# Feed-forward gate and up: one 512-column matmul for both parts of the activations, its halves added on the way out of PSUM

## The chip, the core and the metric

The kernel runs on one core of a Trainium2 chip. The metric is the device time of one execution in microseconds (us), the median of several. The engines named here are TensorE (PE, with its weight loads PEld), VectorE (DVE), ScalarE (ACT), GpSimd (POOL) and SyncE (SP), which issues the loads of the weights.

## The reference, cut to what matters

Two identical layers work on 256 tokens of 1024 channels in float32. Each layer is a feed-forward half step, a mixer of three branches, and a second feed-forward half step:

```python
D_MODEL, SEQ, DEPTH, D_FF = 1024, 256, 2, 2816

def swiglu(x, w_gate, w_up, w_down):
    return (jax.nn.silu(x @ w_gate) * (x @ w_up)) @ w_down

# in each layer
x = x + 0.5 * swiglu(rmsnorm(x, g1), ffn1_gate, ffn1_up, ffn1_down)
x = x + mixers(rmsnorm(x, g_mix))      # sparse attention, S5, dilated attention
x = x + 0.5 * swiglu(rmsnorm(x, g2), ffn2_gate, ffn2_up, ffn2_down)
```

The change touches gate and up of the four feed-forward stages.

## The kernel before

Every float32 product is made of rounded parts. A value is split into a high part, the copy that ACT writes as fp32r, and a low part, the difference that DVE or POOL writes; `mm3` (L105) then adds high times high, high times low and low times high in one PSUM accumulation, three matmuls for each pair of operands.

The weights come as a stream of units of 512 KB. `load_unit` (L206) loads a unit into one of four buffers `raw` by SP; `emit_unit` (L213) has ACT copy it to `wh` (L221) and DVE subtract it to `wl` (L228). There are five buffers each of wh and wl, and `unit()` (L233) sees to it that four units beyond the one in use have been asked for. In the feed-forward stages all wl are DVE's.

`ffn` (L332) goes through D_FF = 2816 in eleven blocks j of 256. Block 0 takes tokens as stationary operand (`tok_mm`). In blocks 1 to 10 the channels are stationary: `chan_mm` (L303) takes two units, each with four of the eight 128-row pieces of the 1024 inputs, and runs over the two halves c of 128 columns. It puts both halves into one PSUM bank "mm" of 512 float32 columns, the first 256 for c = 0, the others for c = 1; each half takes 8 x 3 matmuls of 256 columns (the 256 tokens), with a piece of wh or wl stationary and hTh or hTl, the high and low part of the normalised and transposed activations, moving. One call makes the gate, one the up projection. ACT takes the silu of the gate's bank in one instruction of 512 columns (L367), DVE multiplies the up bank by it (L369), and the product is split into ah by ACT (L370) and al by POOL (L371). Two blocks later `down` multiplies it by w_down into four accumulators (banks "pt" and "sc"), with moving operands of 512 columns. There are two buffers "mm".

In FFN1 `side(j)` adds steps of the set-up of the S5 branch: tables on POOL (L549 to L551), products on POOL (L570, L572) and on DVE (L538 to L540, L576, L578), transposes and small matmuls on PE (L562, L586, L597, L599). These have a lower priority. DVE also computes the parameters of S5 early in layer 0, with one long operation on POOL among them (L444, sp_r).

The order of the instructions on each engine is fixed when the program is built: a scheduler works on the instructions with their priorities and its own notion of their durations. On the chip each engine then takes its instructions in that order, and an instruction that waits holds up those behind it on its engine.

## Time and profile before

| | |
|---|---|
| median of 3 runs | 1362.7 us (1361.65 to 1364.24) |
| profiled execution, its own time | 1364.48 us |
| its span | 1362.7 us |
| mean granted clock of TensorE, share of full speed | 0.994 |
| busy share: PE / DVE / ACT / POOL | 98% / 62% / 51% / 35% |
| HBM read and written | 244.92 MB, 18.58 MB |

The span runs from the first to the last instruction of the profiled execution, and the time of the execution has 1.8 us more around it. A busy share is a mean over all stages of both layers. The four feed-forward stages lie at about 14 to 218 us (FFN1 of layer 0), 504 to 692 (its FFN2), 693 to 893 (FFN1 of layer 1) and 1171 to 1359. Times in rows are counted from the start of the span; a row of a timeline gives the start, the duration, the engine and the line, and in brackets how long the engine had been idle before it and which instruction released it.

### The profile page before, as it was taken

Reading aid. Unit: us, or ns where it says so; the run is one execution under the profiler, and the core shown is the slowest. Engines: PE = TensorE matmul, PEld = TensorE weight load, DVE = VectorE, ACT = ScalarE, POOL = GpSimd, SP = SyncE. Lnnn points to the kernel's source line nnn. Section 1 sums busy time; section 2 is a strip of 40 time slices with the busy share of each in tenths; the row PEclk is TensorE's granted clock in tenths of the full one; section 3 lists DMA queues with packets and bytes.
Section 4 is the critical chain, followed back from the end, with each engine's and each line's share of the span. In section 5 each row is a group of like instructions: output and inputs, shape, how many; then the busy total and the mean of one; then the engine's idle time right before and its main releaser. Section 6 shows DMA issues by size and latency. Waiting matters only on the chain.

```text
span 1362.7 us, 25418 instructions
## 1 busy us (share of the span) xinstructions
PE 1333.8 (98%) x10120; PEld 1257.6 (92%) x10120; DVE 842.1 (62%) x1166; ACT 700.7 (51%) x1018; POOL 474.4 (35%) x333
## 2 busy tenths in 40 slices
PE   8999999999999999999999999999999999999998
PEld 7998997999899979999999999889999999899997
DVE  5696955996434475444586579569864437644443
ACT  5444445687544545444544444456767345444442
POOL 0386514454236531111056125153442556111110
PEclk8999999999899999999999999999999999999999
DMA  8866767666557656666766766676666576466662
GB/s 251 239 197 216 251 213 218 196 184 185 145 157 220 186 176 195 185 186 186 217 187 202 222 202 215 226 231 177 187 199 174 165 220 197 154 189 186 186 186 93
DMA packets 246327, 265.69 MB, mean 195 GB/s; under 512 B 51136, under 2 KB 224192, under 8 KB 246208
## 3 DMA queue, kind: packets, MB, share of 16 engines
q1 hardware_dynamic: 245488, 261.44, 64.0%
q10 hardware_dynamic: 720, 2.62, 0.6%
q8 instruction: 79, 1.29, 0.4%
q14 instruction: 40, 0.33, 0.1%
HBM read 244.92 MB, written 18.58 MB: 193 GB/s over the span
## 4 chain that ended last, share of the span: by engine, by line
PE 76%; DVE 8%; DMA 6%; POOL 5%; ACT 2%; issue 2%; SPq 1%; POOLq 0%; ACTq 0%; DVEq 0%
PE mm L108 18%; PE mm L106 17%; PE mm L107 17%; DVE wl L228 3%; PE pt L108 3%; PE pt L107 3%; PE pt L106 3%; PE sc L108 2%; PE sc L107 2%; PE sc L106 2%; DMA raw<-in_w_in_dram 2%; DMA raw<-in_ffn_gate_dram 1%; ACT wh L221 1%; DMA raw<-in_ffn_down_dram 1%; PE p L900 1%
## 5 line engine op out<-in xcount | busy, mean ns | idle before, releaser
L228 DVE TENSOR_TENSOR wl<-raw,wh 128x1024 fp32r<-128x1024 f32 (+3 forms) x376 | 471.8, 1262 | 338.2 <-ACT wh L221 334.0
L221 ACT ACTIVATE wh<-raw 128x1024 fp32r<-128x1024 f32 (+2 forms) x396 | 414.4, 1048 | 456.9 <-PE mm L107 234.8
L108 PE MATMUL mm<-hTh,wl 128*128 128x256 f32 x1728 | 490.5, 284 | 0.0
L107 PE MATMUL mm<-hTl,wh 128*128 128x256 f32 x1728 | 489.5, 283 | 0.0
L106 PE MATMUL mm<-hTh,wh 128*128 128x256 f32 x1728 | 489.1, 283 | 0.0
L106 PEld LDWEIGHTS mm<-hTh,wh 128*128 128x128 f32 x1728 | 326.6, 189 | 2.2
L107 PEld LDWEIGHTS mm<-hTl,wh 128*128 128x128 f32 x1728 | 325.2, 188 | 1.6 <-issue 0.3
L108 PEld LDWEIGHTS mm<-hTh,wl 128*128 128x128 f32 x1728 | 325.8, 189 | 0.3 <-issue 0.3
L371 POOL TENSOR_TENSOR al<-aa,ah 128x512 fp32r<-128x512 f32 x40 | 68.2, 1706 | 466.1 <-ACT ah L370 466.1
L230 POOL TENSOR_TENSOR wl<-raw,wh 128x384 fp32r<-128x384 f32 (+2 forms) x108 | 144.9, 1347 | 199.6 <-ACT wh L221 166.9
L106 PE MATMUL mm<-wh,hTh 128*128 128x256 f32 (+1 forms) x496 | 143.8, 291 | 0.3 <-ACT hTh L282 0.3
L107 PE MATMUL mm<-wl,hTh 128*128 128x256 f32 (+1 forms) x496 | 142.2, 288 | 0.0
L108 PE MATMUL mm<-wh,hTl 128*128 128x256 f32 (+1 forms) x496 | 141.8, 290 | 0.0
L106 PEld LDWEIGHTS mm<-wh,hTh 128*128 128x128 f32 x496 | 94.8, 191 | 1.4 <-ACT hTh L282 0.5
L107 PEld LDWEIGHTS mm<-wl,hTh 128*128 128x128 f32 x496 | 94.5, 191 | 1.0 <-issue 0.3
L108 PEld LDWEIGHTS mm<-wh,hTl 128*128 128x128 f32 x496 | 93.7, 191 | 1.0 <-issue 0.3
L225 POOL TENSOR_TENSOR wl<-raw,wh 128x512 fp32r<-128x512 f32 x40 | 56.6, 1434 | 51.4 <-ACT wh L221 51.4
L107 PE MATMUL pt<-wl,ah 128*128 128x512 f32 x144 | 56.8, 395 | 1.5 <-DVE wl L228 1.5
L108 PE MATMUL pt<-wh,al 128*128 128x512 f32 x144 | 57.3, 398 | 0.0
L108 PE MATMUL sc<-wh,al 128*128 128x512 f32 x144 | 56.5, 392 | 0.0
L106 PE MATMUL pt<-wh,ah 128*128 128x512 f32 x144 | 56.4, 392 | 0.0
L107 PE MATMUL sc<-wl,ah 128*128 128x512 f32 x144 | 56.3, 391 | 0.0
(311 smaller groups left out, 2073.7 us busy)
## 6 DMA issues: line engine op xcount, KB each, us to landing
raw<-in_w_in_dram SPq DMA_DIRECT2D x100, 512.0 KB, 4.0
raw<-in_ffn_gate_dram SPq DMA_DIRECT2D x88, 512.0 KB, 4.3
raw<-in_ffn_up_dram SPq DMA_DIRECT2D x88, 512.0 KB, 4.6
raw<-in_ffn_down_dram SPq DMA_DIRECT2D x88, 512.0 KB, 4.1
raw<-in_w_out_dram SPq DMA_DIRECT2D x16, 512.0 KB, 3.8
Gd<-xh SPq DMA_DIRECT2D x8, 512.0 KB
Ad<-xl SPq DMA_DIRECT2D x8, 512.0 KB, 4.4
x<-Ad SPq DMA_DIRECT2D x8, 512.0 KB, 4.7
```

Of the source, the lines that this page charges most:

```text
L106: PE.matmul(o, lh, rh, start=start, stop=False)
L107: PE.matmul(o, lh, rl, start=False, stop=False)
L108: PE.matmul(o, ll, rh, start=False, stop=stop)
L221: A.activation(hv, r, AF.Copy)
L225: G.tensor_tensor(lv[:, :, cs], r[:, :, cs], hv[:, :, cs].bitcast(F32), op=ALU.subtract)
L228: V.tensor_tensor(lv[:, :, :c], r[:, :, :c], hv[:, :, :c].bitcast(F32), op=ALU.subtract)
L230: G.tensor_tensor(lv[:, :, c:], r[:, :, c:], hv[:, :, c:].bitcast(F32), op=ALU.subtract)
L371: G.tensor_tensor(al, a, ah.bitcast(F32), op=ALU.subtract)
L900: PE.matmul(bu[:, 32 * g:32 * g + 32], At[:, P * g:P * g + P], U[:, g], start=True, stop=True)
```

## The change

`new_h` makes one tile with the high and the low part of the activations behind each other, so that for each 128-row piece one access pattern [128, 2, 256] reads both. `wide_mm` takes the place of `chan_mm`. It asks for both units first and then runs over the halves c, with a bank of its own for each. For each of the eight pieces it issues one matmul of 512 columns with wh stationary, high and low part moving, into the two halves of the bank, and one of 256 columns with wl stationary and the high part moving into the first half. `gate_out` and `up_out` add the two halves as they leave the bank: an ACT copy of the second half to SBUF, a DVE add of the first; then the silu of 256 columns, or the multiply, in SBUF. In a block that is 64 matmuls for gate and up where there were 96. Each unit is used by two passes. Block 0, down and the mixer stay as they were. In the code after, lines above L250 keep their numbers, the S5 lines are 24 higher (L576 is L600, L578 is L602, L445 is L469).

```diff
     def new_h():
-        return [sb([P, KD, SEQ], F32R, "hTh"), sb([P, KD, SEQ], F32R, "hTl")]
+        both = sb([P, 2, KD, SEQ], F32R, "hT")
+        return [both[:, 0], both[:, 1], None, both]
...
         if t == 1:
-            h.append(last)
+            h[2] = last
...
+    def wide_mm(h, evac):
+        us = [unit() for _ in range(2)]
+        for c in range(2):
+            pq = ps("mm")
+            for kk in range(KD):
+                wh, wl = us[kk // 4]
+                cs = slice(c * P, (c + 1) * P)
+                PE.matmul(pq.rearrange("p (i t) -> p i t", i=2), wh[:, kk % 4, cs], h[3][:, :, kk, :],
+                          start=kk == 0, stop=False)
+                PE.matmul(pq[:, :SEQ], wl[:, kk % 4, cs], h[0][:, kk, :], start=False, stop=kk == KD - 1)
+            evac(c, pq[:, :SEQ], pq[:, SEQ:])
...
-                    pg = chan_mm(h)
-                    A.activation(s, pg, AF.Silu)
-                    pu = chan_mm(h)
-                    V.tensor_tensor(a, pu, s, op=ALU.mult)
+                    def gate_out(c, p0, p1):
+                        A.activation(s[:, c], p1, AF.Copy)
+                        V.tensor_tensor(s[:, c], p0, s[:, c], op=ALU.add)
+                        A.activation(s[:, c], s[:, c], AF.Silu)
+
+                    def up_out(c, p0, p1):
+                        A.activation(a[:, c], p1, AF.Copy)
+                        V.tensor_tensor(a[:, c], p0, a[:, c], op=ALU.add)
+                        V.tensor_tensor(a[:, c], a[:, c], s[:, c], op=ALU.mult)
+
+                    wide_mm(h, gate_out)
+                    wide_mm(h, up_out)
```

The shorter block also gives the scheduler other times, and so the order changes on every engine. Three places follow; the numbers in the names count buffers and differ between the two programs.

PE after, FFN1 of layer 0, block 3: the end of the gate's half c = 0 (bank mm_156), down matmuls of a unit wh_154 and wl_155, and the start of the half c = 1 (mm_157).

```order
L328 MATMUL mm_156_727<-hT_24_124,wl_115_561 128x256
L326 MATMUL mm_156_727<-hT_24_124,wh_114_560 128x512
L328 MATMUL mm_156_727<-hT_24_124,wl_115_561 128x256
L106 MATMUL pt_71_336<-wh_154_723,ah_73_338 128x512
L106 MATMUL sc_70_335<-wh_154_723,ah_73_338 128x512
L106 MATMUL pt_72_337<-wh_154_723,ah_73_338 128x512
L107 MATMUL pt_71_336<-wl_155_724,ah_73_338 128x512
L108 MATMUL pt_71_336<-wh_154_723,al_74_339 128x512
L107 MATMUL sc_70_335<-wl_155_724,ah_73_338 128x512
```

Before, down came after the whole of gate and up; now a part of it stands between the halves of the gate.

DVE in FFN1 of layer 0, around the operation that takes POOL's sp_r (L445, now L469). Before:

```order
L228 TENSOR_TENSOR wl_115_608<-raw_104_536,wh_114_607 128x1024
L462 TENSOR_SCALAR sp_k_131_683<-sp_k_131_683 128x64
L470 TENSOR_TENSOR sp_k_131_683<-sp_im_126_673 128x64
L471 TENSOR_TENSOR sp_den_134_700<-sp_den_134_700,sp_k_131_683 128x64
L472 RECIPROCAL sp_den_134_700<-sp_den_134_700 128x64
L228 TENSOR_TENSOR wl_150_760<-raw_107_566,wh_149_759 128x1024
L228 TENSOR_TENSOR wl_153_790<-raw_110_599,wh_152_789 128x1024
L445 TENSOR_SCALAR sp_xr_128_678<-sp_xr_128_678 128x64
```

After, with the wl of the down unit above as the last row:

```order
L228 TENSOR_TENSOR wl_115_561<-raw_100_458,wh_114_560 128x1024
L469 TENSOR_SCALAR sp_xr_131_637<-sp_xr_131_637 128x64
L228 TENSOR_TENSOR wl_118_567<-raw_105_504,wh_117_566 128x1024
L470 TENSOR_TENSOR sp_r_133_641<-sp_r_133_641,sp_xr_131_637 128x64
L228 TENSOR_TENSOR wl_152_718<-raw_108_510,wh_151_717 128x1024
L490 TENSOR_TENSOR sp_zs_135_652<-sp_r_133_641,sp_zs_135_652 128x64
L492 TENSOR_TENSOR sp_zs_135_652<-sp_r_133_641,sp_zs_135_652 128x64
L514 TENSOR_TENSOR r8_9_77<-sp_r_133_641 128x64
L228 TENSOR_TENSOR wl_155_724<-raw_113_558,wh_154_723 128x1024
```

Before, 19 wl of the program stood ahead of that operation; now there are 16.

DVE in FFN1 of layer 1, blocks 1 to 3. Before, a part with nothing but wl and the multiplies of blocks 1 and 2:

```order
L228 TENSOR_TENSOR wl_1314_8111<-raw_1297_8008,wh_1313_8110 128x1024
L369 TENSOR_TENSOR aa_1292_7976<-mm_1300_8039,silu_1291_7975 128x512
L228 TENSOR_TENSOR wl_1317_8141<-raw_1301_8040,wh_1316_8140 128x1024
L228 TENSOR_TENSOR wl_1321_8173<-raw_1304_8070,wh_1320_8172 128x1024
L228 TENSOR_TENSOR wl_1324_8203<-raw_1312_8108,wh_1323_8202 128x1024
L228 TENSOR_TENSOR wl_1327_8236<-raw_1315_8138,wh_1326_8235 128x1024
L369 TENSOR_TENSOR aa_1310_8106<-mm_1318_8169,silu_1309_8105 128x512
```

After, a part of the same blocks (the stretch from wl_1331 to wl_1386 has twelve wl, four L600 and two L602):

```order
L600 TENSOR_TENSOR xl_1441_8201<-s5C1_1375_7829,s5Q_1403_7989 128x1024
L602 TENSOR_TENSOR xh_1440_8200<-xh_1440_8200,xl_1441_8201 128x1024
L228 TENSOR_TENSOR wl_1359_7738<-raw_1340_7631,wh_1358_7737 128x1024
L228 TENSOR_TENSOR wl_1362_7744<-raw_1349_7683,wh_1361_7743 128x1024
L384 TENSOR_TENSOR silu_1347_7681<-mm_1356_7715,silu_1347_7681 128x256
L600 TENSOR_TENSOR xh_1475_8395<-s5C0_1374_7828,s5Q_1403_7989 128x1024
L389 TENSOR_TENSOR aa_1348_7682<-mm_1363_7747,aa_1348_7682 128x256
L600 TENSOR_TENSOR xl_1476_8396<-s5C1_1375_7829,s5Q_1403_7989 128x1024
L390 TENSOR_TENSOR aa_1348_7682<-aa_1348_7682,silu_1347_7681 128x256
L602 TENSOR_TENSOR xh_1475_8395<-xh_1475_8395,xl_1476_8396 128x1024
L228 TENSOR_TENSOR wl_1367_7792<-raw_1352_7689,wh_1366_7791 128x1024
```

The S5 products L600 and L602 moved here from blocks 5 to 9, and stand ahead of wl and of the adds that free the banks.

## Rows read from the trace of the kernel before

**Rows 1.** The page's first part: busy us, share, instructions.

```profile
PE 1333.8 (98%) x10120; PEld 1257.6 (92%) x10120; DVE 842.1 (62%) x1166; ACT 700.7 (51%) x1018; POOL 474.4 (35%) x333
```

**Rows 2.** Windows, one FFN2 block of layer 0; columns as named in the first line.

```profile
core 0: us, PE busy (x) PEld busy (x) DVE busy (x) ACT busy (x) POOL busy (x), PEclk, DMA share, GB/s
551.00:568.00 17.00, 17.00 (x123) 16.02 (x122) 8.04 (x7) 7.37 (x9) 1.81 (x1) 1.00 0.64 185
```

**Rows 3.** Windows, stretches of FFN1 in layer 0 and layer 1.

```profile
62.00:79.00 17.00, 17.00 (x122) 16.02 (x122) 16.90 (x44) 7.49 (x10) 7.45 (x10) 1.00 0.48 136
...
712.00:723.00 11.00, 11.00 (x95) 11.00 (x94) 11.00 (x7) 5.01 (x7) 11.00 (x6) 1.00 0.75 232
...
828.00:847.00 19.00, 19.00 (x165) 17.67 (x163) 18.04 (x12) 9.27 (x12) 10.44 (x5) 1.00 0.69 226
```

**Rows 4.** Timeline of PE, 256-column matmuls: start us, us, engine, line, operation.

```profile
130.08 0.28 PE L106 MATMUL mm<-hTh,wh 128*128 128x256 f32 x1
...
134.04 0.28 PE L106 MATMUL mm<-hTh,wh 128*128 128x256 f32 x1
```

**Rows 5.** Timeline of PE, 512-column matmuls of down.

```profile
102.03 0.39 PE L106 MATMUL pt<-wh,ah 128*128 128x512 f32 x1
...
104.31 0.39 PE L107 MATMUL sc<-wl,ah 128*128 128x512 f32 x1
```

**Rows 6.** Tile silu: duration in ns, min/median/max, of each form.

```profile
L367 ACT ACTIVATE silu<-mm x40: 575/579/599, 33.8 to 1339.1; 128x512 f32<-128x512 f32 x40
L369 DVE TENSOR_TENSOR aa<-mm,silu x40: 675/691/693, 39.8 to 1342.6; 128x512 f32<-128x512 f32 x40
L356 ACT ACTIVATE silu<-mm x8: 378/382/385, 23.6 to 1182.1; 128x256 f32<-128x256 f32 x8
L357 DVE TENSOR_TENSOR aa<-mm,silu x8: 414/417/427, 26.4 to 1183.8; 128x256 f32<-128x256 f32 x8
```

**Rows 7.** Groups of DVE, FFN2, 551 to 636 us: count, busy us, mean ns.

```profile
L228 DVE TENSOR_TENSOR wl<-raw,wh 128x1024 fp32r<-128x1024 f32 x30 | 36.7, 1225 | 41.1 <-ACT wh L221 40.6
```

**Rows 8.** Groups of DVE, FFN1 of layer 1, 706 to 733 us.

```profile
L228 DVE TENSOR_TENSOR wl<-raw,wh 128x1024 fp32r<-128x1024 f32 x11 | 22.2, 2045 | 0.7 <-ACT wh L221 0.7
...
L364 DVE TENSOR_TENSOR al<-y,ah 128x512 fp32r<-128x512 f32 x1 | 0.7, 678 | 0.0
L558 DVE TENSOR_TENSOR s5D<-s5D,cm 128x128 f32<-128x128 f32 x1 | 0.5, 544 | 0.0
```

**Rows 9.** Timeline of DVE, S5 products in FFN1 of layer 0.

```profile
107.44 2.99 DVE L576 TENSOR_TENSOR xh<-s5C,s5Q 128x1024 f32<-128x1024 f32 x1
112.87 2.29 DVE L576 TENSOR_TENSOR xh<-s5C,s5Q 128x1024 f32<-128x1024 f32 x1 [2.43 <-POOL tab L551]
...
119.77 1.22 DVE L576 TENSOR_TENSOR xl<-s5C,s5Q 128x1024 f32<-128x1024 f32 x1
```

**Rows 10.** Timeline of DVE in layer 1, the wl behind block 0's multiplies.

```profile
707.74 3.71 DVE L228 TENSOR_TENSOR wl<-raw,wh 128x1024 fp32r<-128x1024 f32 x2
```

**Rows 11.** Timeline of PE: first gate matmuls of block 3 (layer 0), block 1 (layer 1).

```profile
55.12 0.28 PE L106 MATMUL mm<-hTh,wh 128*128 128x256 f32 x1
...
704.73 0.28 PE L106 MATMUL mm<-hTh,wh 128*128 128x256 f32 x1
```

**Rows 12.** Timeline of DVE, the operation that takes POOL's sp_r.

```profile
60.59 1.28 DVE L445 TENSOR_SCALAR sp_xr<-sp_xr 128x64 f32<-128x64 f32 x1 [2.13 <-POOL sp_r L444]
```

**Rows 13.** Timeline of POOL, FFN1 of layer 0.

```profile
50.00 10.56 POOL L444 TENSOR_TENSOR sp_r<-sp_eb,sp_xr 128x64 f32<-128x64 f32 x1 [5.05 <-DVE sp_xr L441]
...
85.31 2.94 POOL L570 TENSOR_TENSOR xl<-s5b,s5Q 128x1024 f32<-128x1024 f32 x1
...
111.55 1.28 POOL L551 TENSOR_TENSOR tab<-xh,xl 128x512 f32<-128x512 f32 x1
```

**Rows 14.** Timeline of PE, its waits in FFN1 of layer 0.

```profile
119.91 0.50 PE L107 MATMUL pt<-wl,ah 128*128 128x512 f32 x1 [0.76 <-DVE wl L228]
...
122.49 0.50 PE L107 MATMUL pt<-wl,ah 128*128 128x512 f32 x1 [0.76 <-DVE wl L228]
```

**Rows 15.** The page's fifth part, ACT's copies of the weights.

```profile
L221 ACT ACTIVATE wh<-raw 128x1024 fp32r<-128x1024 f32 (+2 forms) x396 | 414.4, 1048 | 456.9 <-PE mm L107 234.8
```

## The prediction

> **What bounds the kernel now.** I read the busy shares first: PE is busy 98% of the span, DVE 62%, ACT 51% [rows 1]. Then I read the same shares stage by stage, because a mean says nothing of a stage. In the second feed-forward stage (FFN2) of a layer a block of 17.00 us has PE busy for all of it, DVE for 8.04 and ACT for 7.37 [rows 2]: PE alone bounds it, and nothing else is near. In the first stage (FFN1), which carries the S5 set-up as side work, PE is full too, but DVE is busy 16.90 of 17, 11.00 of 11 and 18.04 of 19 in the stretches shown [rows 3]. There DVE is a second bound just below the first, and it makes the low parts of the weights (wl, L228) without which PE can't go on. So the change has two halves with opposite signs: what it takes from PE counts in all four stages, what it adds to DVE counts where DVE has no room.
>
> **What PE gains.** Eleven triples of three 256-column matmuls take 134.04 - 130.08 = 3.96 us, 0.360 a triple and 0.120 a matmul [rows 4]. Ten 512-column matmuls take 104.31 - 102.03 = 2.28 us between the starts shown, 0.228 each [rows 5]. The new pair (one wide, one narrow) costs 0.228 + 0.120 = 0.348, so a pair saves 0.0125 (0.2275 taken for the wide). Gate and up of one block have 2 x 2 x 8 = 32 pairs, there are 10 changed blocks in each of 4 stages, hence 1280 pairs and **-16.0 us**. The trace has no matmul whose moving side reads two separate runs of 256, as the wide one does. Its bounds are the 0.2275 of a plain 512 and 0.240, two 256s, at which the gain is nothing; columns alone (512 / 2.4 GHz = 0.2133) would give -34. I take 0.2275, the row with the same number of columns.
>
> The Trainium skill's "TensorE: Matmul & The Clock Gate" (Back-to-back issue gap) puts the pitch of a warm matmul at N/2.4 ns plus about 2.5. By that a pair saves 2.5 ns against a triple, and the gain is an estimated 3.2 us instead of 16. The rows disagree: 0.120 and 0.2275 lie 13 and 14 ns above streaming.
>
> **What the way out costs.** One silu of 512 (0.579) and one multiply of 512 (0.691) become, for each half, a PSUM copy and a silu of 256 on ACT beside the up copy (0.382 by the 256-column silu), and two adds and a multiply of 256 on DVE (0.417 by the 256-column multiply) [rows 6]. ACT: 6 x 0.382 - 0.579 = +1.7 us a block; DVE: 6 x 0.417 - 0.691 = +1.8. In FFN2 that is DVE 9.9 and ACT 9.1 of 16.6: hidden. The banks too: each half has its own, and the order puts nine down matmuls (9 x 0.2275 = 2.0 us) or a whole other half between two uses. I cost it at nothing in FFN2; without that cover it would be the 1.2 us of copy, add and silu per half. New_h as one tile and the moved h[2] cost nothing.
>
> **What it costs in FFN1.** The scheduler answers the shorter blocks by placing the S5 side work earlier, and DVE runs strictly in the order that front shows.
>
> *Layer 1, blocks 1 to 3.* Between the wl named 1331 and the one named 1386 DVE now has 12 wl, 12 of the new 256-wide operations, four L600 and two L602 (L576 and L578 before) and two small ones. Before, this stretch had no L576 or L578. A wl takes 1.225 us alone [rows 7] but 2.045 here, where POOL computes beside it [rows 8]; L576 took 2.99 and 2.29 beside POOL, 1.22 alone [rows 9]. Sum: 12 x 2.045 = 24.5, 12 x 0.417 = 5.0, 4 x 2.29 = 9.2, 2 x 1.22 = 2.4, small ones 0.68 + 0.54 [rows 8], together 42.3. It starts at 707.74 [rows 10], so wl 1386 is there at 750.0 less the last two small operations, 749.2. PE starts block 1 at 704.73 [rows 11] and reaches the first matmul that wants wl 1386 after nine half passes of 8 x 0.348 (25.0), 27 down matmuls at 0.2275 (6.1) and 20 transposes at not over 0.12 (2.4): 738.2. PE waits **+11.0 us** in all. With wl and L600 at 1.22, as without POOL, DVE would be done at 735.0 and the wait is nothing; with L600 behind POOL's last table as well it is some 13.
>
> *Layer 0, blocks 3 to 5.* DVE's L445 waits until 60.59 for POOL's sp_r [rows 12], which takes 10.56 us from 50.00 [rows 13]. Before, 19 wl stood ahead of it, now 16 (as L469). So the wl of the down unit that PE wants between the two gate halves of block 3 comes three wl and four small operations behind that wait: 60.6 + 1.3 + 3 x 1.22 + 0.7 = 66.2. PE, which started block 3 at 55.12 [rows 11], would be there at 54.3 + 2.8 + 0.7 = 57.8. That is 8 us, or 4 if POOL can start sp_r some 4 us earlier because DVE's inputs for it no longer stand behind L558. In block 4 the wl of the next down unit stands behind three other wl and four S5 products of DVE; two or three of these at the 2.3 to 3.0 us of rows 9 in place of 1.22 make it up to 5 late. In block 5 an L600 waits for POOL's last table, which was ready at 111.55 + 1.28 = 112.8 and now has two more L570 of up to 2.94 ahead of it [rows 13]; behind that L600 stands an add which frees the bank that PE wants. PE is late by then, so 0 to 5. Sum 4 to 18; I take **+11**, and take off the 1.5 that PE already lost here [rows 14].
>
> *Later blocks of both layers.* 18.04 + 1.8 = 19.8 of DVE stands against 18.6 of PE [rows 3], 1.2 us in each of two such blocks: **+2.5**, between 0 and 7.
>
> **Sum.** -16.0 + 11.0 + 11.0 - 1.5 + 2.5 = +7.0 on the profiled execution's 1364.5, so 1371.5. That execution lies 1.8 above the median of the runs, 1362.7; on the median it is 1369.7, and I forecast **1370**. SP's weight loads move with the buffers that they fill and are cheap (DMA share 0.64 in rows 2); POOL's al waits for ACT as before.
>
> **Rivals.**
> (A) *The cover holds: faster, about 1351.* DVE is slow beside POOL only while POOL reads; if POOL's chain ends early or its turns fall elsewhere, wl costs 1.225 and the wait in layer 1 goes to 0, in layer 0 to the 4 us of sp_r: -16 + 4 = -12, 1351. For it: rows 7, and that PE lost only two gaps of 0.76 in the old schedule [rows 14] although DVE was full. Against it: POOL has the same chain to run, two products earlier. It decides below some 1.4 us a wl.
> (B) *The wide matmul saves nothing: about 1384.* If its two runs are read like two matmuls the pair costs 0.360, or if the fixed part is small the saving is a few us; the stalls shrink little with blocks that stay long: 1362.7 + 23 - 2 = 1384, the 2 being five stalled blocks whose PE time is 0.4 longer. Against it: the 512-column rows [rows 5]; nothing in the trace has that pattern. The skill's page named above would put it within 3 us of this.
> (C) *FFN2 stalls too: about 1382.* A weight unit now serves two passes and is given back one pass later; ACT's copy of the next (1.05 us) already waits for PE in 235 us of the profile [rows 15], and then DVE needs 1.22. Walking the block with these durations leaves about 1 us at the two tightest units. If each is 0.3 us late, 20 blocks x 0.6 = 12 more. For it: the margin was several us before. Against it: DVE and ACT have 40% free there [rows 2].
>
> **How the numbers follow.** A measurement of this kernel can tell some 0.2% from no change, so the borders are 1360.0 and 1365.4. The forecast has 0.50, its own range 1362 to 1378 (net stalls of 15 to 31 against the gain of 16): 0.46 slower, 0.04 same. A has 0.32 with a range of 1347 to 1364: 0.25 faster, 0.07 same. B has 0.06, C 0.12, both slower. Faster 0.25, same 0.11, slower 0.64. As cases of both signs hold the chance, the range for 8 in 10 reaches into A and into C: 1349 to 1384.
>
> **What would show it.** Right, if the profile after has pairs at 0.348 and FFN2 blocks of 16.6 us, and PE gaps released by DVE's wl or by the adds of L384 and L389 in FFN1, near 58 to 66, 80 to 120 and 712 to 752 us, some 20 in sum. FFN2 blocks of 17.0 speak for B, of 17.2 or gaps behind ACT's wh in FFN2 for C. Wrong about FFN1 if PE shows no gaps there and wl stands at 1.2 to 1.4. The least sure step is layer 0, where three waits hang on one another.

## The result and the profile after

| | before | after |
|---|---|---|
| median | 1362.81 us (1361.65 to 1364.24, 4 runs) | 1405.97 us (1404.06 to 1407.5, 4 runs) |
| ratio | | 1.0299, 95% interval 1.028 to 1.0318 |
| span of the profiled execution | 1362.7 us | 1405.1 us |
| mean granted clock, share of full speed | 0.994 | 0.983 |

The change makes the kernel 3.0% slower, 43 us. The direction was forecast, the size was not: 1370, with 1384 as the upper end.

The first part of the profile page of the kernel after, to be read beside [rows 1]:

```profile
PE 1348.8 (96%) x8840; PEld 1201.4 (86%) x8840; DVE 910.8 (65%) x1366; ACT 758.6 (54%) x1218; POOL 469.4 (33%) x333
```

PE has 1280 matmuls less and is busy 15.0 us longer. It also stands idle longer: 1405.1 - 1348.8 = 56.3 us against 28.9, so 27.4 more. Both need an answer, since only the second is a wait. The first is more than it looks: the pairs take some 12 us of work away (below), so the busy time is some 27 us longer than the work accounts for.

Where the time is lost can be read from the start of the last update of x in each stage (the fourth L324 before, L340 after; the last stage runs to the end of the span), in us a stage:

| | FFN1, layer 0 | mixer | FFN2 | FFN1, layer 1 | mixer | FFN2 |
|---|---|---|---|---|---|---|
| before | 218.3 | 285.6 | 188.7 | 200.3 | 278.2 | 191.6 |
| after | 242.1 | 278.1 | 192.6 | 219.9 | 281.6 | 190.7 |
| difference | +23.8 | -7.5 | +3.9 | +19.6 | +3.4 | -0.9 |

The two FFN1 stages carry the whole loss. The mixers have the same code in both kernels. In the profiled executions of all kernels of this document they take 276 to 286 us in layer 0 and 278 to 285 in layer 1, so what they differ by here is within the scatter of one execution.

*FFN2.* The windows of one block, as in [rows 2]:

```profile
551.00:567.70 16.70, 16.70 (x89) 14.32 (x89) 9.63 (x12) 8.88 (x14) 1.29 (x1) 1.00 0.60 186
```

PE is full, and DVE and ACT have 40% and more free at the added work. How long a block takes shows in the copy that ACT makes once in each, the first two rows before and the last two after:

```profile
557.18 0.61 ACT L370 ACTIVATE ah<-aa 128x512 fp32r<-128x512 f32 x1
574.18 0.61 ACT L370 ACTIVATE ah<-aa 128x512 fp32r<-128x512 f32 x1
...
564.20 0.62 ACT L394 ACTIVATE ah<-aa 128x512 fp32r<-128x512 f32 x1
580.90 0.62 ACT L394 ACTIVATE ah<-aa 128x512 fp32r<-128x512 f32 x1
```

A block takes 16.70 us where it took 17.00. So in a block the change does what it says, 0.30 us and not 0.40. But the stage of layer 0 got longer, at its end. The timeline of PE there:

```profile
698.71 0.39 PE L108 MATMUL pt<-xh,al 128*128 128x512 f32 x1
701.73 0.64 PE L106 MATMUL pt<-xh,ah 128*128 128x512 f32 x1 [2.63 <-ACT ah L394]
```

The last block has no next pass behind which its copy, add, multiply and copy could hide, so down waits for ah at their end. In layer 1 no such stop came.

*FFN1.* The waits of PE, the longest groups (before, it waited for wl twice, [rows 14]; columns: total us, times, longest):

```profile
PE y L280 <- DVE xn L276: 11.4, 6, 4.1
PE mm L326 <- DVE silu L384: 10.3, 7, 4.3
PE pt L107 <- DVE wl L228: 8.1, 6, 3.9
...
PE mm L328 <- DVE wl L228: 3.2, 1, 3.2
```

L384 is the new add of the gate, which frees the bank; L280, the transposes of the next norm, waits mostly at the end of the FFN1 stages. Four of the stops, two in layer 0 and two in layer 1:

```profile
84.06 0.77 PE L107 MATMUL pt<-wl,ah 128*128 128x512 f32 x1 [3.92 <-DVE wl L228]
238.22 1.09 PE L280 MATMUL y<-ident,xn 128*128 128x128 f32 x4 [4.09 <-DVE xn L276]
738.29 0.50 PE L326 MATMUL mm<-hT,wh 128*128 128x512 f32 x1 [2.97 <-DVE silu L384]
767.31 0.58 PE L328 MATMUL mm<-hT,wl 128*128 128x256 f32 x1 [3.21 <-DVE wl L228]
```

How another one, of 4.25 us, comes about shows in layer 0 on three engines. POOL:

```profile
116.06 1.29 POOL L575 TENSOR_TENSOR tab<-xh,xl 128x512 f32<-128x512 f32 x1
117.31 1.29 POOL L395 TENSOR_TENSOR al<-aa,ah 128x512 fp32r<-128x512 f32 x1
118.56 3.33 POOL L596 TENSOR_TENSOR xh<-xh,xl 128x1024 f32<-128x1024 f32 x1
```

DVE:

```profile
117.39 2.30 DVE L600 TENSOR_TENSOR xh<-s5C,s5Q 128x1024 f32<-128x1024 f32 x1 [2.44 <-POOL tab L575]
119.61 3.36 DVE L228 TENSOR_TENSOR wl<-raw,wh 128x1024 fp32r<-128x1024 f32 x1
122.89 0.41 DVE L384 TENSOR_TENSOR silu<-mm,silu 128x256 f32<-128x256 f32 x1
```

PE:

```profile
118.72 0.39 PE L108 MATMUL sc<-wh,al 128*128 128x512 f32 x1
123.36 0.79 PE L326 MATMUL mm<-hT,wh 128*128 128x512 f32 x1 [4.25 <-DVE silu L384]
```

DVE waits 2.44 us for POOL's last table, computes the S5 product, makes a wl at 3.36 us beside POOL's L596, and only then the add of 0.41 us for which PE has stood since 119.1. The add itself is cheap; its place in the row is what costs.

In layer 1 DVE has next to no gap from 730 to 775 us. Its groups there (count, busy us, mean ns, and idle time before them):

```profile
L228 DVE TENSOR_TENSOR wl<-raw,wh 128x1024 fp32r<-128x1024 f32 x12 | 21.7, 1848 | 0.0
L600 DVE TENSOR_TENSOR xl<-s5C,s5Q 128x1024 f32<-128x1024 f32 x2 | 5.8, 2877 | 0.0
L600 DVE TENSOR_TENSOR xh<-s5C,s5Q 128x1024 f32<-128x1024 f32 x2 | 4.4, 2202 | 0.0
L390 DVE TENSOR_TENSOR aa<-aa,silu 128x256 f32<-128x256 f32 x4 | 4.4, 1099 | 0.1
L602 DVE TENSOR_TENSOR xh<-xh,xl 128x1024 f32<-128x1024 f32 x2 | 3.4, 1707 | 0.0
L384 DVE TENSOR_TENSOR silu<-mm,silu 128x256 f32<-128x256 f32 x5 | 2.1, 411 | 0.0
```

With the small groups left out here the sum is some 45 us in a window of 45.

*What follows a stop.* The windows around two of them; the number before the last two is the granted clock:

```profile
119.00:123.40 4.40, 0.15 (x2) 0.04 (x1) 4.40 (x4) 0.06 (x1) 2.89 (x1) 0.80 0.75 229
123.40:127.00 3.60, 3.60 (x11) 3.12 (x12) 3.56 (x5) 3.60 (x5) 0.00 (x0) 0.50 0.78 287
127.00:131.00 4.00, 4.00 (x20) 3.22 (x20) 2.95 (x4) 1.50 (x3) 0.00 (x0) 0.81 0.94 294
735.00:738.40 3.40, 0.43 (x4) 0.20 (x3) 3.40 (x4) 0.44 (x2) 3.40 (x2) 1.00 0.46 148
738.40:742.00 3.60, 3.60 (x15) 3.09 (x16) 3.56 (x3) 1.92 (x3) 3.60 (x3) 0.65 0.52 162
```

PE comes back at 1.2 GHz, the lower of its two levels, and is "busy" for all of 123.40 to 127.00 with 11 matmuls. So a part of the longer busy time is time at the lower clock. In the feed-forward stages, the program's first norm left aside, the trace of the kernel after has seven stretches with a granted clock of 0.50, and each lies at one of seven stops: those that end at 84.06, 123.36, 238.22, 701.73, 738.29, 767.31 and 928.20, of 2.63 to 4.25 us. The kernel before has no such stretch there while PE works, and none of PE's shorter stops has one here. The seven give 15.4 us of full-speed work away, 1.8 of it while PE stood still anyway. Over the whole span the clock costs (1 - 0.983) x 1405.1 = 23.9 us, against (1 - 0.994) x 1362.7 = 8.2; what is lost while PE works is some 14 us more than before.

### The profile page after: what moved, and what is told of

Its sections match the earlier page's. It is cut to its first block, busy times and chain, and to the rows that moved or that the text cites. A ratio compares the mean times of both kernels' runs of the same rounds, so it can differ in the third digit from the quotient of the medians.

```text
span 1405.1 us, 23200 instructions
## 1 busy us (share of the span) xinstructions
PE 1348.8 (96%) x8840; PEld 1201.4 (86%) x8840; DVE 910.8 (65%) x1366; ACT 758.6 (54%) x1218; POOL 469.4 (33%) x333
## 4 chain that ended last, share of the span: by engine, by line
PE 71%; DVE 8%; DMA 8%; POOL 5%; issue 4%; ACT 4%; SPq 0%; DVEq 0%; ACTq 0%; POOLq 0%
PE mm L326 17%; PE mm L328 9%; PE mm L106 7%; PE mm L107 7%; PE mm L108 7%; DVE wl L228 3%; PE pt L106 3%; PE pt L107 3%; PE pt L108 2%; PE sc L106 2%; PE sc L107 2%; PE sc L108 2%; DMA raw<-in_ffn_gate_dram 2%; DMA raw<-in_w_in_dram 2%; ACT wh L221 2%
## 5 line engine op out<-in xcount | busy, mean ns | idle before, releaser
L228 DVE TENSOR_TENSOR wl<-raw,wh 128x1024 fp32r<-128x1024 f32 (+3 forms) x376 | 460.1, 1234 | 284.8 <-ACT wh L221 276.7
L326 PE MATMUL mm<-hT,wh 128*128 128x512 f32 x1280 | 460.5, 398 | 10.4 <-DVE silu L384 10.3
L328 PE MATMUL mm<-hT,wl 128*128 128x256 f32 x1280 | 363.7, 284 | 3.2 <-DVE wl L228 3.2
L326 PEld LDWEIGHTS mm<-hT,wh 128*128 128x128 f32 x1280 | 242.9, 190 | 67.9 <-DVE silu L384 13.3
L328 PEld LDWEIGHTS mm<-hT,wl 128*128 128x128 f32 x1280 | 243.2, 190 | 7.4 <-DVE wl L228 3.5
L106 PE MATMUL mm<-wh,hT 128*128 128x256 f32 (+1 forms) x496 | 144.8, 293 | 0.3 <-ACT hT L284 0.3
L107 PE MATMUL mm<-wl,hT 128*128 128x256 f32 (+1 forms) x496 | 143.2, 290 | 0.0
L108 PE MATMUL mm<-wh,hT 128*128 128x256 f32 (+1 forms) x496 | 142.5, 291 | 0.0
L108 PE MATMUL mm<-hT,wl 128*128 128x256 f32 x448 | 126.9, 283 | 0.0
L107 PE MATMUL mm<-hT,wh 128*128 128x256 f32 x448 | 126.6, 283 | 0.0
L106 PE MATMUL mm<-hT,wh 128*128 128x256 f32 x448 | 126.4, 282 | 0.0
L106 PEld LDWEIGHTS mm<-wh,hT 128*128 128x128 f32 x496 | 95.8, 193 | 1.4 <-ACT hT L284 0.5
L107 PEld LDWEIGHTS mm<-wl,hT 128*128 128x128 f32 x496 | 95.4, 193 | 1.2 <-issue 0.5
L108 PEld LDWEIGHTS mm<-wh,hT 128*128 128x128 f32 x496 | 94.7, 192 | 1.0 <-issue 0.3
L107 PEld LDWEIGHTS mm<-hT,wh 128*128 128x128 f32 x448 | 84.3, 188 | 0.3 <-issue 0.3
L108 PEld LDWEIGHTS mm<-hT,wl 128*128 128x128 f32 x448 | 84.3, 188 | 0.3 <-issue 0.3
L106 PEld LDWEIGHTS mm<-hT,wh 128*128 128x128 f32 x448 | 84.4, 188 | 0.0
```

Source lines behind the costliest of these rows:

```text
L106: PE.matmul(o, lh, rh, start=start, stop=False)
L107: PE.matmul(o, lh, rl, start=False, stop=False)
L108: PE.matmul(o, ll, rh, start=False, stop=stop)
L228: V.tensor_tensor(lv[:, :, :c], r[:, :, :c], hv[:, :, :c].bitcast(F32), op=ALU.subtract)
L326: PE.matmul(pq.rearrange("p (i t) -> p i t", i=2), wh[:, kk % 4, cs], h[3][:, :, kk, :], start=kk == 0, stop=False)
L328: PE.matmul(pq[:, :SEQ], wl[:, kk % 4, cs], h[0][:, kk, :], start=False, stop=kk == KD - 1)
```

## The experiments

All kernels start from the one after; each time is a median, each ratio is against runs of the kernel before on the same chip.

### Which stages: wide in FFN2 only, and in FFN1 only

`wide` is a new argument of `ffn`, true for one of the two stages of a layer.

```diff
-                    wide_mm(h, gate_out)
-                    wide_mm(h, up_out)
+                    if wide:
+                        wide_mm(h, gate_out)
+                        wide_mm(h, up_out)
+                    else:
+                        pg = chan_mm(h)
+                        A.activation(s, pg, AF.Silu)
+                        pu = chan_mm(h)
+                        V.tensor_tensor(a, pu, s, op=ALU.mult)
```

> Wide matmuls in the two FFN2 stages only; FFN1 as in the kernel before. Theory: the 43 us were lost in FFN1 (23.8 us in layer 0, 19.6 in layer 1 by the times of the last update of x), where DVE holds PE up and the clock falls behind each stop, and in FFN2 the pair saves only some 5 ns. Then FFN1 is as before and FFN2 gives what it gave in the kernel after: +3.9 and -1.3 us, in all 1362 to 1367, with FFN2 blocks of 16.7 us. Rival, the wide pass itself costs wherever it stands (two runs read as two matmuls, PSUM halves, banks held): the 43 us go with the matmuls, half of them in FFN2, 1380 to 1385.

Measured: 1371.1 (1362.1 to 1376.1, 10 runs), ratio 1.0047, interval 1.0025 to 1.0069. The median lies 4 us above what was expected, and the runs spread over 14 us. The clock goes with it: 1362.08 has a granted clock of 0.995, 1376.11 one of 0.986, and 0.9% of 1365 is 12 us. In the one execution that was profiled (1363.9) the FFN1 stages are as before, 218.9 and 200.1, and one stop is left in FFN2:

```profile
682.28 0.50 PE L106 MATMUL pt<-xh,ah 128*128 128x512 f32 x1 [2.70 <-ACT ah L400]
```

In the 7.8 us behind this stop the granted clock is 1.00. So where the clock fell in the longer runs is not shown.

> The other half: wide matmuls in the two FFN1 stages only. Theory (the loss is in FFN1): 1400 to 1406, with PE stops behind the adds (L384) and behind wl in both FFN1 stages as in the kernel after. Rival (the wide pass costs everywhere): 1380 to 1385. The changes of the two halves should add up to that of the whole, 43 us.

Measured: 1406.2 (one run), FFN1 stages 240.6 and 220.1, FFN2 stages as before. The loss is in FFN1: 41.8 us against the runs before of the same job, 1364.4, where FFN2 alone has 6.7. Together that is 48.5 us and not the 43 of the whole, but FFN1's part rests on a single run. The wide pass by itself does not cost 20 us wherever it stands.

### The wide matmul reading one run

```diff
-        both = sb([P, 2, KD, SEQ], F32R, "hT")
-        return [both[:, 0], both[:, 1], None, both]
+        both = sb([P, KD, 2, SEQ], F32R, "hT")
+        return [both[:, :, 0], both[:, :, 1], None, both]
...
-                PE.matmul(pq.rearrange("p (i t) -> p i t", i=2), wh[:, kk % 4, cs], h[3][:, :, kk, :],
+                PE.matmul(pq.rearrange("p (i t) -> p i t", i=2), wh[:, kk % 4, cs], h[3][:, kk],
```

> As the kernel after, but the high and low part of the activations lie beside each other for each 128-row piece, so the wide matmul reads one run of 512 columns in place of two of 256. In the kernel after a wide matmul took 0.234 us to the next start and the narrow one 0.121. If the two runs are what costs the 0.234, it falls to 0.2275 (a plain 512): 1280 x 0.0065 = 8 us less, 1398, and FFN2 blocks of 16.5 us. If it is the alternation of wide and narrow (or the banks), nothing moves: 1404 to 1408, blocks of 16.7.

Measured: 1405.1, ratio 1.0296 (1.0271 to 1.0321), blocks of 16.7 us. Two runs of 256 in place of one of 512 cost nothing that can be seen here.

### Taking the way out apart

The loss can come from the frame (both units first, halves outside, a bank for each half), from the wide matmul, from the copies, or from the adds. Four kernels separate them.

```diff
 # frame alone, three matmuls
-                PE.matmul(pq.rearrange("p (i t) -> p i t", i=2), wh[:, kk % 4, cs], h[3][:, :, kk, :],
-                          start=kk == 0, stop=False)
-                PE.matmul(pq[:, :SEQ], wl[:, kk % 4, cs], h[0][:, kk, :], start=False, stop=kk == KD - 1)
+                mm3(pq[:, :SEQ], wh[:, kk % 4, cs], wl[:, kk % 4, cs],
+                    h[0][:, kk, :], h[1][:, kk, :], kk == 0, kk == KD - 1)
...
 # frame alone, and frame with the wide matmul
-                        A.activation(s[:, c], p1, AF.Copy)
-                        V.tensor_tensor(s[:, c], p0, s[:, c], op=ALU.add)
-                        A.activation(s[:, c], s[:, c], AF.Silu)
+                        A.activation(s[:, c], p0, AF.Silu)
...
-                        A.activation(a[:, c], p1, AF.Copy)
-                        V.tensor_tensor(a[:, c], p0, a[:, c], op=ALU.add)
-                        V.tensor_tensor(a[:, c], a[:, c], s[:, c], op=ALU.mult)
+                        V.tensor_tensor(a[:, c], p0, s[:, c], op=ALU.mult)
```

> The three 256-column matmuls as before, but in the new frame: both units asked for first, the half c as the outer loop, a bank for each half, silu and multiply on 256 columns straight from the bank. No wide matmul, no copy, no add. PE has the work of the kernel before. The order of this kernel moves the S5 products of layer 1 ahead just as the wide one does (the first stands before the third wl pair of block 1). Theory A, the frame and the order that it brings cause the stops in FFN1: 1380 to 1395, with stops behind wl in FFN1. Theory B, the copies and adds cause them: within 5 us of before, 1358 to 1368.

Measured: 1377.4, ratio 1.0095 (1.0073 to 1.0117). Between the two theories: the frame alone costs 13 us against the runs before of the same job (1364.4), with 221.6 and 205.6 us in FFN1.

> As the kernel after, with the wide matmul, but nothing is added on the way out: the silu and the multiply of 256 columns read the first half of the bank alone, so the product of the high weights with the low activations is left out of the result. No copy and no add, PE's work is that of the kernel after. The frame alone (three matmuls, halves) gave 1377. Theory A, the copies and adds on ACT and DVE make the rest of the loss: 1366 to 1374, the frame's 1377 less what the wide pair saves (1280 x 5 to 6 ns = 7). Theory B, PE that runs faster simply outruns DVE's wl: 1385 to 1400, with stops behind wl left.

Measured: 1381.3, ratio 1.0123 (1.0101 to 1.0145). Neither range holds it. In FFN2 the wide matmul gives what it should, 375.7 us for both stages against the frame's 382.0. In FFN1 it takes 443.6 against 427.2. PE, which asks for its weights sooner, does run into DVE's wl: 9.0 us in five stops, against 2.5 in one with the frame alone. But that is not all of it, since the norm at the ends of the two stages is waited for as well, 4.3 and 3.0 us against 1.0 each.

```profile
PE y L280 <- DVE xn L276: 10.3, 6, 4.3
PE pt L107 <- DVE wl L228: 7.4, 4, 3.7
...
PE mm L328 <- DVE wl L228: 1.6, 1, 1.6
```

The third of the four has the copies, but no adds (the edit is shown against the second):

```diff
+                        A.activation(s[:, c], p1, AF.Copy)
                         A.activation(s[:, c], p0, AF.Silu)
...
+                        A.activation(a[:, c], p1, AF.Copy)
                         V.tensor_tensor(a[:, c], p0, s[:, c], op=ALU.mult)
```

> As the kernel after with the ACT copies of the second halves, but without the DVE adds: silu and multiply read the first half, the copy is overwritten, so the product of the high weights with the low activations is left out of the result. Without copies and adds it was 1381, with both 1405. Theory, DVE's adds (four of 0.42 us a block, in the order of a full engine) make the difference: 1380 to 1387. Rival, ACT's copies make it, since they stand ahead of the copies of the weights: 1397 to 1405.

Measured: 1390.0, ratio 1.0194 (1.0157 to 1.0232), between the two. On this way from one kernel to the next the copies cost 9 us and the adds 16; 8.6 of the 16 lie in FFN1 and 6.1 in FFN2.

The fourth has three matmuls with copies and adds (the matmul of the low activations writes the bank's second half; the edit is shown against the kernel after, whose wide and narrow matmul it replaces):

```diff
+    def mm3h(o0, o1, lh, ll, rh, rl, start, stop):
+        PE.matmul(o0, lh, rh, start=start, stop=False)
+        PE.matmul(o1, lh, rl, start=False, stop=False)
+        PE.matmul(o0, ll, rh, start=False, stop=stop)
...
+                mm3h(pq[:, :SEQ], pq[:, SEQ:], wh[:, kk % 4, cs], wl[:, kk % 4, cs],
+                    h[0][:, kk, :], h[1][:, kk, :], kk == 0, kk == KD - 1)
```

> The counterpart: three 256-column matmuls as before, high weights times low activations going into the second half of the bank, then copied and added as in the kernel after. Frame, copies and adds are those of the kernel after, only the wide matmul is missing. Theory A (copies and adds): near 1405 plus the 7 us that the pair saved, 1405 to 1415. Theory B (PE outruns wl): near the frame's 1377, up to 1388.

Measured: 1416.9, ratio 1.0389 (1.0371 to 1.0406). That is 2 us above the range of theory A, whose reading holds: copies and adds cost 40 us on the frame, without any wide matmul. Together, with the times of the FFN1 and of the FFN2 stages (sums of both layers, from the profiled execution):

| frame | wide | copies | adds | time | FFN1 | FFN2 |
|---|---|---|---|---|---|---|
| - | - | - | - | 1362.8 | 418.6 | 380.3 |
| yes | - | - | - | 1377.4 | 427.2 | 382.0 |
| yes | yes | - | - | 1381.3 | 443.6 | 375.7 |
| yes | yes | yes | - | 1390.0 | 453.4 | 377.2 |
| yes | yes | yes | yes | 1406.0 | 462.0 | 383.3 |
| yes | - | yes | yes | 1416.9 | 462.0 | 387.6 |

The parts don't add up, and that is a finding too. In FFN1 the wide matmul costs 16 us where DVE still has some room, and nothing where copies and adds have filled it, 462.0 with or without it (244.9 and 217.1 without, 242.1 and 219.9 with). That DVE sets the time there is the likely reading; each of these kernels also has an order of its own.

### The bank set free by ACT

```diff
                         A.activation(s[:, c], p1, AF.Copy)
-                        V.tensor_tensor(s[:, c], p0, s[:, c], op=ALU.add)
+                        A.activation(a[:, c], p0, AF.Copy)
+                        V.tensor_tensor(s[:, c], a[:, c], s[:, c], op=ALU.add)
                         A.activation(s[:, c], s[:, c], AF.Silu)
```

> As the kernel after, but ACT copies both halves of the gate's bank to SBUF and DVE adds them there, so the gate's banks come free behind ACT and no longer behind DVE's add. DVE has as many operations, ACT one copy of 0.38 us more for each half (0.8 us a block). In the profile after PE stopped 10.3 us in 7 places behind L384, that add. Theory, the bank that waits for a full DVE is a large part of the loss: those stops go, 1390 to 1397. Rival, DVE's time is what counts, whatever the bank waits for: the stops turn up behind wl, 1403 to 1410.

Measured: 1389.6, ratio 1.0193 (1.015 to 1.0235), just below the range of the theory. The stops behind the gate's add are gone, and 16 us with them, although ACT has more to do and DVE no less. In the profiled execution 8.7 us of it lie in FFN1 of layer 0 and 6.7 in the two FFN2 stages. But in layer 1 FFN1 stays at 219.6 us (219.9). The waits of the whole run:

```profile
PE mm L326 <- DVE aa L390: 9.3, 5, 3.7
PE mm L328 <- DVE wl L228: 5.5, 2, 4.1
```

L390 is in this kernel the add of up, which was L389 in the kernel after, and it still frees up's banks in DVE's order. Two of these stops, of 3.7 and 2.1 us, lie in layer 1; two others there are behind wl, of 1.2 and 1.4 us. So the gate's bank, waiting for DVE's order, did cost time in layer 0 and in FFN2, whose stop of 2.63 us is gone. In layer 1 the wait went from the gate's bank to up's, and no run had ACT free both: whether bank or full engine counts there stays open.

### Side work a block later

```diff
-                with tc.high_priority(offset=TO):
-                    next(gen, None)
+                if j >= 3:
+                    with tc.high_priority(offset=TO):
+                        next(gen, None)
```

> As the kernel after, but the S5 side work is handed out from block 3 on and not from block 2. Theory: the stops of layer 1 at blocks 2 and 3 come from S5 products that the scheduler puts ahead of wl and adds; handed out one block later they lie one block later, DVE still has them to do in as many blocks, and the total moves by less than 8 us: 1398 to 1410. Rival, only their place at the very start of the stage hurts, where no weights are ready yet: FFN1 of layer 1 falls from 219.9 to 205, the total to 1390.

Measured: 1415.1 (one run), 5 us over the range. FFN1 takes 247.3 and 224.2 us. But the run tests neither theory, since the edit did not move what it was meant to move: in layer 1 DVE has the same L600 and L602 between the same wl and adds as in the kernel after, and PE the same stops, 2.95 us at 744.75 and 3.19 at 773.78 (the stage starts 6.2 us later than in the kernel after). What is new lies at the end of the stages, where with fewer blocks left PE waits for copies of weights by ACT, 10.7 us in all against 1.1:

```profile
PE pt L106 <- ACT xh L221: 10.7, 4, 6.2
```

### Towards a version that keeps the gain

Wide in FFN2 only, and there not in the last block (the edit is shown against the run with wide in FFN2 only):

```diff
-                    if wide:
+                    if wide and j < NB - 1:
```

> Wide matmuls in FFN2 alone and there not in the last block of a stage. With wide in all of FFN2 one stop of 2.7 us was left, the last down of layer 0 behind ACT's ah, and the runs spread from 1362 to 1376 with the granted clock at 0.995 to 0.986. Theory: that stop sits at the end of the chain copy, add, multiply, copy of the last block, and the clock falls behind it in most runs; without it FFN2 of layer 0 takes 186 to 187 us in place of 191.1, of layer 1 189, the runs lie together: 1357 to 1362. Rival, the spread is of FFN2's whole (weights just in time): still 1362 to 1376.

Measured: 1360.9 (1358.1 to 1365.3), ratio 0.9978 (0.9965 to 0.9992): faster by 0.2%. FFN2 takes 186.3 and 189.1 us against 188.7 and 191.6, and PE has no stop of over 0.6 us in it. So the stop at the end of the stage went with the last block's new way out. The runs still spread by 7 us, as those of the kernel before do (1361.3 to 1368.0 in the same job), not by 14.

Then, on top of it and in place of the loop that issues a wide and a narrow matmul in turn:

```diff
+            for kk in range(KD):
+                PE.matmul(pq.rearrange("p (i t) -> p i t", i=2), us[kk // 4][0][:, kk % 4, cs], h[3][:, :, kk, :],
+                          start=kk == 0, stop=False)
+            for kk in range(KD):
+                PE.matmul(pq[:, :SEQ], us[kk // 4][1][:, kk % 4, cs], h[0][:, kk, :], start=False, stop=kk == KD - 1)
```

> As the run with wide matmuls in FFN2 but not in its last blocks (1360.9), with the eight wide matmuls of a half ahead of its eight narrow ones, where they alternated. In the profiles a wide one takes 0.234 to the start of the narrow one behind it; 512-column matmuls of down in a row take 0.2275. If the alternation costs that, the pair falls from 0.355 to 0.348, FFN2 blocks from 16.70 to 16.5 us, 18 blocks x 0.2 = 4 us: 1355 to 1359. If not, 1359 to 1363 and blocks of 16.7.

Measured: 1356.8 (1354.4 to 1360.6), ratio 0.9947 (0.9929 to 0.9965), the fastest of all. The time lies in the range of the theory, and the theory is wrong: the blocks still take 16.69 us. The timeline of PE shows the eight of each kind as one row:

```profile
602.96 2.02 PE L325 MATMUL mm<-hT,wh 128*128 128x512 f32 x8
604.81 1.12 PE L328 MATMUL mm<-hT,wl 128*128 128x256 f32 x8
605.77 0.62 PE L325 MATMUL mm<-hT,wh 128*128 128x512 f32 x2
```

(604.81 - 602.96) / 8 = 0.231 a wide and 0.96 / 8 = 0.120 a narrow one, 0.351 a pair; in turn it was 0.350 (eight pairs from 599.90 to 602.70 in the kernel after), not 0.355. FFN2 takes 186.2 and 189.2 us, as in the run above. The medians of the two lie 4 us apart, and their profiled executions 9.5 us, all of it in stages that they share: FFN1 of layer 0 (216.9 against 219.8) and the mixers (281.6 and 279.4 against 285.2 and 282.3), with granted clocks of 0.996 and 0.991. So nothing shows that the order of the matmuls made the difference. In FFN2 both are 2.4 to 2.5 us better than before in each layer, close to the 0.30 us for each of 18 blocks.

The last one puts the release of the gate's bank by ACT on top (`gate_out` as above).

> The same, and the gate's banks come free behind two ACT copies, DVE adding from SBUF. In FFN2 PE waits for nothing in the blocks, so the bank's release should not matter there: as the run without it, within 2 us. Rival: the later way out of the bank shows at the ends of the stages or in the pitch, 3 us or more in either direction.

Measured: 1360.1 (1357.1 to 1363.8), ratio 0.9966 (0.9953 to 0.998). FFN2 takes 186.5 and 189.6 us: no gain there, as expected. The time is 3.3 us over the run before it, which was to be within 2 us; the profiled executions differ by 0.7 us in FFN2, and the rest lies in stages that the edit leaves alone (the runs have granted clocks of 0.991 to 0.995 here and 0.992 to 0.996 there).

## Why the prediction was right or wrong

**What bounds: right.** FFN2 by PE alone, FFN1 by DVE just below PE. The four kernels that leave FFN1 alone are the only ones within 0.6% of before.

**PE's gain, -16: mis-sized.** A wide matmul takes 0.231 in a row of eight, not the 0.2275 taken from [rows 5]; the pair is 0.351, the block 0.30 shorter, and 40 blocks give -12. Neither the two runs nor the alternation is the cause; it stays open. The estimate by the page of the Trainium skill ("TensorE: Matmul & The Clock Gate", Back-to-back issue gap), a gain of 3.2 us, was further off than the row.

**The way out: two of three prices right, one place missed.** The copies took 0.380 and 0.366 (0.382 forecast), the adds 0.417. But the multiply L390 now reads two operands from SBUF. Durations in ns, min/median/max:

```profile
L384 DVE TENSOR_TENSOR silu<-mm,silu x80: 405/417/426, 32.6 to 1383.7; 128x256 f32<-128x256 f32 x80
L390 DVE TENSOR_TENSOR aa<-aa,silu x80: 404/425/1844, 37.8 to 1391.5; 128x256 f32<-128x256 f32 x80
```

The add with one operand in PSUM never leaves its 0.42; the multiply goes to 1.84 beside POOL, and the mean of four in layer 1 (730 to 775 us) was 1.10, where I had put 0.417. The Trainium skill, "SBUF — State Buffer" (Who interferes with whom), says that a DVE instruction with two SBUF inputs contends with a GpSimd instruction that reads SBUF and one with at most one does not; these two rows agree. And "I cost it at nothing in FFN2" holds for the blocks, not for the last one of a stage, which has no next pass over it.

**Layer 1, +11: the mechanism right, the size 3 us too large.** DVE is full from 730 to 775, with the twelve wl, four L600 and two L602 that the order showed. PE's gaps there are 0.61, 2.97, 1.09 and 3.21, together 7.9.

**Layer 0, +11: the sum near, by luck; one of its three parts wrong.** The stop behind sp_r, priced at 8 us and at 4 if POOL started early, was 0.16. POOL did start 4 us earlier, and PE came 5 us later than I had put it (62.8 against 57.8), so that the wl was nearly there.

```profile
46.17 10.80 POOL L468 TENSOR_TENSOR sp_r<-sp_eb,sp_xr 128x64 f32<-128x64 f32 x1 [13.01 <-DVE sp_xr L465]
...
63.17 0.50 PE L107 MATMUL pt<-wl,ah 128*128 128x512 f32 x1 [0.16 <-DVE wl L228]
```

The wl of block 4 (3.92 us) and the add behind POOL's last table (4.25) came where they were forecast. Small stops that were not forecast, 0.3 to 1.5 us each, take the place of sp_r; with them it is 13.8. The 2.5 of the later blocks were nothing.

**The step that failed: each stop was priced at its own length, and the ends of the stages at nothing.** With what was measured the sum has -12 for the pairs and +20.2 for the stops that it names (13.8 + 7.9 - 1.5), against -16 and +23. That alone gives 1371, near the forecast; two terms are absent, which the rivals and the range left out too.

First, the ends of the stages: 5.3 against 3.0 us of gaps in front of the norm in layer 0, 5.2 against 2.8 in layer 1, and 3.4 at the end of FFN2, 8 together. The last is the way out of the last block, which "I cost it at nothing in FFN2" forgot. At the end of FFN1 PE has the same six matmuls of down left in both kernels; what comes later is the norm. Its sums of squares are ACT's L264 before (first two rows) and L266 after:

```profile
212.30 0.63 ACT L264 ACTIVATE junk<-x 128x512 bf16<-128x512 f32 x1 [1.49 <-DVE x L324]
213.06 0.63 ACT L264 ACTIVATE junk<-x 128x512 bf16<-128x512 f32 x1
...
232.31 0.61 ACT L266 ACTIVATE junk<-x 128x512 bf16<-128x512 f32 x1
234.01 1.06 ACT L221 ACTIVATE wh<-raw 128x1024 fp32r<-128x1024 f32 x1 [0.99 <-DMA raw<-in_w_in_dram]
234.97 0.61 ACT L266 ACTIVATE junk<-x 128x512 bf16<-128x512 f32 x1
```

After, the second stands behind a copy of weights that waits for its load, 2.7 us after the first where it was 0.8. So what costs there is ACT's order and the load in it, and not the matmuls or the way out.

Second, and largest, **the clock after a stop, some 14 us**. The trace of before already had the price; windows around a wait in its mixer:

```profile
349.00:352.40 3.40, 1.01 (x10) 0.78 (x8) 2.21 (x4) 2.52 (x5) 1.00 (x1) 0.96 0.48 78
352.40:359.20 6.80, 6.70 (x32) 6.70 (x33) 1.65 (x4) 1.26 (x3) 0.00 (x0) 0.52 0.83 270
```

6.8 us at half speed behind a stop of 2.5 are 3.4 more lost. The Trainium skill, "TensorE: Matmul & The Clock Gate" (HAM oscillation — how this bites in real kernels), says that gaps in PE's work bring the clock down and that the matmuls behind them pay; the windows after 123.40 and 738.40 agree with it, at 0.50 and 0.65, while the stop of 2.70 in the run with wide in FFN2 only had no such stretch behind it.

Together: -12 + 20 + 8 + 14 = 30 of the 42 us of span. The other 12 are not assigned. They lie in FFN1, which lost 43.4 us: PE's idle time there grew by 25.8, the clock takes some 12 and the pairs give 6 back. A part may be waits shorter than a matmul's modelled end, which don't show as idle: between 118.72 and 123.36 PE started nothing for 4.64 us, 0.23 of which a matmul takes, and 4.25 of it is shown as idle.

**The rivals.** A (the cover holds) fell: wl took 1.85 in layer 1, above the 1.4 at which it was to decide. B (the wide saves nothing) fell: 0.30 us a block. C (FFN2 stalls) fell for the blocks. B and C ended nearer to 1406 than the forecast did, but not for their reasons.

**What stays open.** Why a wide matmul takes 0.231; what the clock costs was read from windows and from runs of one kernel at two clocks, not set by an experiment, and why some stops have a slow stretch behind them and others not; 12 of the 42 us; and the order itself, which every one of these edits changes, was never held fixed. So what the table puts down to the frame, the copies and the adds includes the order that came with each.

## What to carry to other kernels

A saving on the bounding engine is paid for on the engine next to it: read the stage where that one is fullest, not its mean, and ask in which row the new instruction will stand and what is held (here a PSUM bank) until it is done. A short operation that frees a resource should not stand in the order of a full engine; freeing the gate's bank by ACT gave 16 of the 43 us back. And a stop of PE can cost more than its length (here seven stops of 2.6 to 4.3 us, 25 together, had some 14 more behind them), so price stops with the clock behind them. Look at the ends of the stages apart from the blocks, and make a change like this only in the stages and blocks that have cover: in FFN2 without its last block it gained 4.9 us of the two stages.

## What the runs showed of the hardware that was not expected

A moving operand of two separate runs of 256 columns costs the same as one of 512 (1405.1 against 1406.0 in all), and eight 512-column matmuls in a row take 0.231 each here where down's take 0.228. The runs of one kernel, with wide in FFN2 only, spread over 14 us, and the granted clock went with them (1362.1 at 0.995, 1376.1 at 0.986; 0.9% is 12 us); the one that was profiled has a single stop of over 1 us in the stages that had been changed, of 2.7. A DVE operation on two operands in SBUF took 0.40 to 1.84 us for the same 256 columns, and the gate's add, with one operand in PSUM, 0.405 to 0.426.
